# Expert results stored by an indirect store with one index per row, into a table that lies over scratch arrays

## The chip, the cores and the metric

The kernel runs on one core of a Trainium2 chip, in one launch. The metric is the device time of an execution in microseconds (us). The kernel before took 1542.76 us, the median of three runs (1533.67, 1542.76 and 1543.29).

## What is computed

One layer of a hybrid decoder runs over 1024 prompt tokens and 64 sample tokens (8 sequences of 8), 1088 tokens of width 1024 in all. A projection feeds eight RWKV-7 heads (a recurrence per token) and eight heads of dilated windowed attention; an output projection and a residual follow. Then comes the part that the change is about:

- A router picks for each token one of 4 groups of experts and in it 2 of 8 gated-MLP experts, with two weights. The layer adds the two weighted results: `acc + c[:, None] * ((silu(hf @ wg) * (hf @ wu)) @ wd)` for each of the 32 experts, where `c` is zero for tokens that did not choose it. 1088 tokens with 2 choices make 2176 pairs of a token and an expert.
- After that a per-layer embedding is gated and added, and a last RMSNorm gives the output.

## The kernel before, in words

Phases 1 to 3 hold the projection, the recurrence and the attention. Their scratch arrays in device memory are made in `dram` (L79): among them `XV`, `KB`, `BB`, `BV`, `AA` and `GG`, each 4 x 128 x 1088 float32, written slab by slab in phase 1 (L366, L367, L373, L424, L430, L438) and read in the recurrence, the last time at about 711 us. All these transfers are issued by the SP queue.

Phase 4 (`phase4_`, L1356) does the output projection, the norm and the routing. Each expert owns 96 slots (`CAP`). The tokens of an expert get its slots in order of their rank, from slot 0 up; matmuls build `pidx`, a 96 x 32 table that holds for each slot and expert the token's number minus 2048, and 0 where the slot has no token. Line L1563 adds 2048 and makes the integer table `idx`: a slot without a token then holds 2048, which is over the last row of `HN` (the normed tokens, 1088 rows of 1024). `cnt` (L1566) counts the tokens of each expert. `overflow` (L1729) reads the counts and branches: only if an expert has more than 96 tokens does the block behind it run.

Phase 5 runs the 32 experts. Its parts are made in `moe_fns` (L1604):

- `gather(e)` (L1609) issues an indirect load on the POOL queue: 96 rows of `HN` by column `e` of `idx` into a tile of 96 partitions, row by partition. It has a bounds check; a row whose index is out of range is not loaded.
- `xt` transposes the gathered rows and splits them into a high and a low part; `gu` does the gate and up matmuls, `act` the activation, `ht` transposes its result, `down(e, j)` does the down matmul for one half of the columns.
- `out(e, j)` (L1657) copies half a result from PSUM to the tile `y` on ACT. After the second half, L1663 issues on the POOL queue a plain store of all 96 rows to rows 96e to 96e+95 of `YE`, a table of 3072 rows of 1024 float32 (L1239). `y` has three buffers.

The weights of an expert (`load_w`, `load_d`: gate and up in four transfers of 512 KB, down in one of 1024 KB) are issued on the SP queue some three experts ahead, into buffers that come free when ACT and DVE have split the weights of an earlier expert. The order of phase 5 is written out by hand in `phase5` (L1680): between `ordered = True` and `ordered = False` each engine and each queue keeps the order of the program. In the turn of expert e the POOL queue gets the store of expert e - 2 (`out(e - 2, 1)`, L1693) and then the gather of expert e + 3 (L1695), and nothing else. In the other phases a planner orders the instructions by priority and by a model of their times. Waits are made from what an instruction reads and writes: of a transfer, the part of a table that its access pattern names.

Phase 6 (`phase6`, L1797) loads for each tile of tokens the residual and, with two indirect loads by `slot` from `YE` (L1810), the two results of each token; it adds them by weight (L1819), and does the gated embedding and the last norm. The matmuls of the embedding (`embed`, L1568) run beside the first of these loads. `slot` names only rows of slots that were given to a token.

## Time and profile before

| | |
|---|---|
| median of three runs | 1542.76 us (1533.67 to 1543.29) |
| the profiled execution's own time | 1534.7 us |
| its span, first to last instruction | 1533.0 us |
| PE busy in the span | 1373.5 us, 90% |
| DVE, ACT, POOL busy | 957.5, 749.3, 375.6 us |
| mean granted TensorE clock | 0.951 |
| bytes read from and written to device memory | 276.00 MB, 104.05 MB |

The profile is one execution as the hardware profiler saw it. Busy times are sums over an engine's instructions. Windows are in us from the start of the span. The 32 stores of L1663 lie between 1078.8 and 1378.4 us.

### The profile page before, as it was taken

To read this page: it belongs to the slowest core of one execution; us is meant where nothing else is said; L and a number is where in the kernel's file an instruction comes from. 1 tells how busy PE (TensorE), PEld (TensorE's weight loads), DVE (VectorE), ACT (ScalarE), POOL (GpSimd) and SP (SyncE) were. 2 spreads that over 40 slices of the span, in tenths; PEclk is the share of its full clock that TensorE was granted. 3 is DMA by queue.
4 is the path that set the end of the run, shared out by engine and by line. 5 is a ranking of instruction groups with operands and counts; after the bars stand their busy time and mean duration, and the time that the engine had idled before them with its cause. 6 is when DMAs were issued, how large, how long until landed. Compare 5 with 4: busy or idle time off the path is not lost. (4 is left out here: it accounts for less than half of the span.)

```text
span 1533.0 us, 24768 instructions
## 1 busy us (share of the span) xinstructions
PE 1373.5 (90%) x9127; PEld 1129.0 (74%) x9128; DVE 957.5 (62%) x2146; ACT 749.3 (49%) x1368; POOL 375.6 (25%) x391
## 2 busy tenths in 40 slices
PE   4899999989789889995799889996999999988996
PEld 4888999989767767775576667884676666656884
DVE  7523664272148675834557554656898899886664
ACT  5544453321244444533355563333887888783322
POOL 8104453000121222343223331111111112102221
PEclk9999999999888989797999999997999999999998
DMA  6145566999578465339888755555999999997551
GB/s 212 42 159 170 170 194 196 318 313 311 160 190 221 132 183 162 115 88 158 137 185 248 260 167 177 198 200 197 382 391 384 388 388 390 372 367 241 188 171 69
DMA packets 254271, 344.63 MB, mean 225 GB/s; under 512 B 103918, under 2 KB 183088, under 8 KB 253617
## 3 DMA queue, kind: packets, MB, share of 16 engines
q1 hardware_dynamic: 209536, 286.37, 57.0%
q0 software_dynamic: 43296, 52.02, 12.2%
q10 hardware_dynamic: 1312, 4.59, 0.8%
q8 instruction: 74, 1.21, 0.3%
q14 instruction: 53, 0.43, 0.1%
HBM read 276.00 MB, written 104.05 MB: 248 GB/s over the span
## 5 line engine op out<-in xcount | busy, mean ns | idle before, releaser
L270 PE MATMUL pj<-hT_hi,wh 128*128 128x384 f32 (+1 forms) x600 | 199.2, 334 | 4.7 <-DVE lora L278 2.7
L270 PE MATMUL pj<-hT_hi,wl 128*128 128x384 f32 (+1 forms) x600 | 199.0, 332 | 0.0
L270 PE MATMUL pj<-hT_lo,wh 128*128 128x384 f32 (+1 forms) x600 | 198.4, 331 | 0.0
L270 PEld LDWEIGHTS pj<-hT_hi,wh 128*128 128x128 f32 x600 | 113.8, 190 | 6.6 <-DVE lora L278 3.0
L270 PEld LDWEIGHTS pj<-hT_hi,wl 128*128 128x128 f32 x600 | 114.0, 190 | 2.4 <-issue 2.2
L270 PEld LDWEIGHTS pj<-hT_lo,wh 128*128 128x128 f32 x600 | 114.2, 190 | 0.6 <-issue 0.2
L690 DVE TENSOR_TENSOR ftmp<-At,X 128x60 f32<-128x60 f32 (+24 forms) x248 | 57.2, 243 | 54.7 <-DMA At<-ABd 18.2
L1611 POOL DMA_INDIRECT x<-HN,idx x32 | 38.3, 1198 | 204.8 <-PE p4t L1624 195.5
L55 DVE TENSOR_TENSOR dl<-draw,dh 128x1024 fp32r<-128x1024 f32 x66 | 80.0, 1216 | 3.6 <-ACT dh L54 3.6
L1095 PE MATMUL pS<-k,q 128*128 128x512 f32 (+2 forms) x192 | 53.7, 393 | 21.7 <-DMA q<-QP 21.1
L54 ACT ACTIVATE dh<-draw 128x1024 fp32r<-128x1024 f32 x66 | 69.0, 1050 | 8.0 <-DMA draw<-in_w_down_dram 8.0
L55 DVE TENSOR_TENSOR wl<-w,wh 128x1024 fp32r<-128x1024 f32 x25 | 35.2, 1408 | 45.0 <-ACT wh L54 44.2
L692 DVE TENSOR_TENSOR X<-X,ftmp 128x60 f32<-128x60 f32 (+24 forms) x248 | 60.4, 256 | 4.2
L779 POOL TENSOR_TENSOR s<-S,pc 128x512 f32<-128x512 f32 x16 | 16.9, 1055 | 180.5 <-DVE S L798 74.3
L1098 DVE CUSTOM_DVE_ANT_0 s<-pS,bias 128x512 f32<-128x512 f32 (+2 forms) x96 | 50.2, 554 | 11.6 <-PE pS L1095 7.9
L1122 ACT ACTIVATE pt<-pxt 128x512 f32<-128x512 f32 (+3 forms) x64 | 32.4, 514 | 50.7 <-PE pxt L1118 50.5
L1118 PE MATMUL pxt<-ident,s 128*128 128x128 f32 x288 | 48.2, 291 | 9.4 <-DVE pt L1120 5.9
L1107 ACT ACTIVATE s<-s,nm 128x128 f32<-128x128 f32 (+7 forms) x64 | 49.2, 770 | 13.3 <-DVE nm L1103 6.8
L1095 PEld LDWEIGHTS pS<-k,q 128*128 128x128 f32 x192 | 32.4, 204 | 30.7 <-issue 22.7
L1348 PE MATMUL p4y<-dh,hh 128*96 128x512 f32 x128 | 54.0, 422 | 0.7 <-ACT hh L54 0.7
L1348 PE MATMUL p4y<-dh,hl 128*96 128x512 f32 x128 | 50.5, 395 | 0.0
L1348 PE MATMUL p4y<-dl,hh 128*96 128x512 f32 x128 | 50.3, 393 | 0.0
(682 smaller groups left out, 3836.0 us busy)
## 6 DMA issues: line engine op xcount, KB each, us to landing
wraw<-in_w_gate_dram SPq DMA_DIRECT2D x64, 512.0 KB
wraw<-in_w_up_dram SPq DMA_DIRECT2D x64, 512.0 KB
draw<-in_w_down_dram SPq DMA_DIRECT2D x32, 1024.0 KB
out_dram<-in_cache_k_win_dram SPq DMA_DIRECT2D x16, 1016.0 KB
out_dram<-in_cache_v_win_dram SPq DMA_DIRECT2D x16, 1016.0 KB
w<-in_w_in_dram SPq DMA_DIRECT2D x25, 512.0 KB
kc<-in_cache_k_win_dram SPq DMA_DIRECT2D x48, 256.0 KB
vc<-in_cache_v_win_dram SPq DMA_DIRECT2D x48, 256.0 KB
```

Of the source, the lines that this page charges most:

```text
L54: self.hi = self.o(e.activation(hi, src, AF.Copy) if e is nc.scalar else e.tensor_copy(hi, src))
L55: return self.o((lo_eng or nc.vector).tensor_tensor(lo, src, hi.bitcast(F32), op=ALU.subtract))
L270: nc.tensor.matmul(p[:, :nn], a[:, k, :], b[:, k, n0:n0 + nn], start=(m == 0), stop=(m == 23))
L690: nc.vector.tensor_tensor(o, At[:, t, t + 1:32][:, :, None].to_broadcast([128, m, c]), X[:, t, None, 0:c].to_broadcast([128, m, c]), op=AL ...
L692: nc.vector.tensor_tensor(X[:, t + 1:32, 0:c], X[:, t + 1:32, 0:c], o, op=ALU.add)
L1095: nc.tensor.matmul(ps[:, :n], q[:, a, i * 128:(i + 1) * 128], k[:, c0:c0 + n], start=(a == 0), stop=(a == 1))
L1098: nc.vector.tensor_tensor_reduce(s[:, c0:c0 + n], ps[:, :n], bias[:, bo:bo + n], 1.0, -3e38, ALU.add, ALU.max, m)
L1107: ex = nc.scalar.activation(s[:, :nb * 128], s[:, :nb * 128], AF.Exp, bias=nm, accum_out=den)
L1118: nc.tensor.transpose(px[:, b, :], s[:, (b0 + b) * 128:(b0 + b + 1) * 128], self.ident)
L1122: nc.scalar.activation(pt[:, b0:b0 + m, :], px[:, :m, :], AF.Copy)
L1348: self.o(self.nc.tensor.matmul(p, a[x][:, k, :], w, start=(k == 0 and q == 0), stop=(k == kn - 1 and q == 2)))
L1611: d = nc.gpsimd.indirect_dma_start(out=X[e][:n], out_offset=None, in_=self.HN, in_offset=bass.IndirectOffsetOnAxis(ap=self.idx[:, e:e + 1] ...
```

## The change

Three things are done.

1. `YE` is no table of its own any more. The six scratch arrays of the recurrence become slabs of one array `R6` of 6 x 4 x 128 x 1088 float32 (3342336 numbers), and `YE` is a view of its first 3072 x 1024 numbers, which covers the first five slabs and part of the sixth.
2. The constants get a column with the partition's number. After `idx`, two small DVE operations on 96 x 32 build `row`: the slot's row in `YE` (partition + 96 e), plus 3072 where `pidx` is not negative, which is where the slot has no token.
3. The store of L1663 becomes an indirect store on the same queue, with the rows of `y` as source, column `e` of `row` as the index and a bounds check at 3071: a row with an index of 3072 or more is not stored. Its destination, as the instruction names it, is the whole of `YE`.

```diff
-        self.XV = t("XV", [4, 128, T])
+        self.R6 = t("R6", [6, 4, 128, T])
+        self.XV = self.R6[0]
...
-        self.KB = t("KB", [4, 128, T])
-        self.BB = t("BB", [4, 128, T])
+        self.KB = self.R6[1]
+        self.BB = self.R6[2]
...
-        self.BV = t("BV", [4, 128, T])
-        self.AA = t("AA", [4, 128, T])
-        self.GG = t("GG", [4, 128, T])
+        self.BV = self.R6[3]
+        self.AA = self.R6[4]
+        self.GG = self.R6[5]
...
+    row[:, 149] = j
...
-        self.YE = d.tile([NE * CAP, D], F32, name="YE")
+        self.YE = self.R6.rearrange("s p q t -> (s p q t)")[0:NE * CAP * D].rearrange("(r c) -> r c", c=D)
...
+        self.row = c4.tile([CAP, NE], I32, name="row")
...
-        irk, tid = rc[:, 172:172 + CAP], rc[:, 268:277]
+        irk, tid, row = rc[:, 172:172 + CAP], rc[:, 268:277], rc[:, 277:278]
...
         nc.vector.tensor_scalar(self.idx, pidx[:CAP, 0:NE], float(FREE), None, op0=ALU.add)
+        free = p4.tile([CAP, NE], F32, name="free")
+        nc.vector.tensor_scalar(free, pidx[:CAP, 0:NE], 0.0, float(NE * CAP), op0=ALU.is_ge, op1=ALU.mult)
+        nc.vector.scalar_tensor_tensor(self.row, free, row[:CAP], ist[:CAP], op0=ALU.add, op1=ALU.add)
...
-                self.o(nc.gpsimd.dma_start(self.YE[e * n:e * n + n, :], y[:n]))
+                self.o(nc.gpsimd.indirect_dma_start(out=self.YE, out_offset=bass.IndirectOffsetOnAxis(ap=self.row[:, e:e + 1], axis=0),
+                                                    in_=y[:n], in_offset=None, bounds_check=NE * CAP - 1, oob_is_err=False))
```

## Rows read from the trace of the kernel before

**Rows 1.** The page: the span in 40 slices (PE busy, DMA busy and GB/s).

```profile
PE   4899999989789889995799889996999999988996
...
DMA  6145566999578465339888755555999999997551
GB/s 212 42 159 170 170 194 196 318 313 311 160 190 221 132 183 162 115 88 158 137 185 248 260 167 177 198 200 197 382 391 384 388 388 390 372 367 241 188 171 69
```

**Rows 2.** Busy times by stretch; the columns are given in the first line, the last three being the granted TensorE clock, the busy share of the DMA engines and GB/s.

```profile
core 0: us, PE busy (x) PEld busy (x) DVE busy (x) ACT busy (x) POOL busy (x), PEclk, DMA share, GB/s
...
1097.00:1106.20 9.20, 9.20 (x48) 6.54 (x47) 8.99 (x12) 8.28 (x13) 1.57 (x3) 1.00 1.02 385
1078.77:1333.73 254.96, 241.61 (x1197) 169.10 (x1196) 231.11 (x285) 213.46 (x312) 46.76 (x52) 1.00 1.02 386
1380.00:1460.00 80.00, 76.46 (x349) 61.44 (x350) 52.46 (x64) 28.63 (x51) 24.78 (x23) 0.97 0.66 217
```

**Rows 3.** The chain of work that ended last, in order of time (start us, us, what), in the middle and at the end of phase 5.

```profile
1097.49 2.76 PE p4g L1348 x12
...
1106.64 2.77 PE p4g L1348 x12
...
1248.62 15.35 DMA wraw<-in_w_up_dram
...
1302.69 14.96 DMA wraw<-in_w_up_dram
...
1378.38 3.49 DMA YE<-y
1381.93 0.52 issue
1382.50 0.16 issue
1382.66 2.70 POOL y L1810
1385.36 0.30 issue
1385.66 4.44 DMA y<-YE,slot
```

**Rows 4.** The waits of the SP queue from 1078 to 1385 us: in total, how often, the longest.

```profile
SPq L1305 <- DVE hl L55: 70.8, 27, 3.8
SPq L1305 <- DMA draw<-in_w_down_dram: 59.9, 21, 3.8
```

**Rows 5.** DMA traffic from 1078 to 1332 us by queue: packets, MB, share of the time of 16 engines (q0 is POOL's queue, q1 SP's), and two of the issues with KB each and the median us from issue to landing.

```profile
q1 hardware_dynamic: 21658, 80.29, 82.1%
q0 software_dynamic: 5824, 17.59, 19.4%
...
YE<-y POOLq DMA_DIRECT2D x26, 384.0 KB, 7.3
x<-HN,idx POOLq DMA_INDIRECT x26, 7.7
```

**Rows 6.** POOL's queue in order of time (start us, us, what): the gather and the store of one turn, the gather of the next turn, and the last two stores.

```profile
1096.38 0.97 POOL L1611 DMA_INDIRECT x<-HN,idx  x1 [7.21 <-PE p4t L1624]
1098.42 0.55 POOL L1663 DMA_DIRECT2D YE<-y  x1 [1.06 <-ACT y L1661]
1105.53 0.97 POOL L1611 DMA_INDIRECT x<-HN,idx  x1 [6.56 <-PE p4t L1624]
...
1371.52 0.51 POOL L1663 DMA_DIRECT2D YE<-y  x1 [7.98 <-ACT hh L54]
1378.38 0.51 POOL L1663 DMA_DIRECT2D YE<-y  x1 [6.35 <-ACT y L1661]
```

**Rows 7.** DMA traffic in two short stretches, after the gather issued at 1096.38 and before any packet of the store issued at 1098.42: from 1100.2 to 1100.3, then from 1100.2 to 1100.72 us.

```profile
DMA packets 23, 0.03 MB, mean 287 GB/s; under 512 B 16, under 2 KB 16, under 8 KB 23
...
q0 software_dynamic: 14, 0.00, 7.9%
...
q0 software_dynamic: 43, 0.06, 31.7%
```

**Rows 8.** GB/s in 40 slices of 0.5 us each, from 1290 to 1310 us.

```profile
GB/s 418 418 418 410 451 385 426 418 369 426 344 352 361 303 401 320 385 475 410 402 410 410 459 418 385 377 410 377 344 320 320 320 246 270 352 401 426 426 426 401
```

**Rows 9.** All gathers of L1611, then all stores of L1663: duration of an issue in ns (least, median, most), and us from the issue to the landing.

```profile
L1611 POOL DMA_INDIRECT x<-HN,idx x32: 956/975/2007, 1052.4 to 1331.7; - x32
...
DMA to landing us min/median/max: 4.5/7.7/9.6
...
L1663 POOL DMA_DIRECT2D YE<-y x32: 505/548/559, 1078.8 to 1378.4; - x32
...
DMA to landing us min/median/max: 3.5/7.2/8.8
```

**Rows 10.** DVE in order of time at the end of phase 4: the line that makes `idx`, and the last one before the branch; and the first gather on POOL.

```profile
1051.97 0.17 DVE L1563 TENSOR_SCALAR idx<-p4g 96x32 int32<-96x32 f32 x1
...
1052.22 0.13 DVE L1741 CAST ci<-mx 1x1 int32<-1x1 f32 x1
...
1052.44 1.06 POOL L1611 DMA_INDIRECT x<-HN,idx  x1 [7.02 <-DVE ci L1741]
```

**Rows 11.** The SP queue in phases 1 to 2 (four writes to four parts of one scratch table, then the next load), and the stores of `X` with their median us to landing.

```profile
276.65 3.76 SPq L627 DMA_DIRECT2D ABd<-LAB  x4
280.51 0.65 SPq L600 DMA_DIRECT2D bb<-BB  x1
...
X<-x POOLq DMA_DIRECT2D x7, 512.0 KB, 2.9
```

## The prediction, made before the changed kernel was run

> **What bounds the kernel now.** I read the page's slices first: PE is busy almost throughout, but from slice 29 on (1073 to 1380 us) the DMA engines are full as well, at 367 to 391 GB/s [rows 1]. That is phase 5, the stage of the change. The table by stretch then says how close the two limits lie. Where the weights were there in time, one turn of an expert is 9.15 us, from 1097.49 to 1106.64, and PE is busy in all of it [rows 2, 3]. From the first store at 1078.77 to the one at 1333.73 there are 26 turns in 254.96 us, 9.81 each, with PE busy 241.61 us, 9.29 a turn, and a DMA share of 1.02 [rows 2]. So over this stretch transfers, not PE, set the pace; the chain of waits names whom it waits for, the weight loads, with single pieces of 15 us [rows 3]. The SP queue's own waits add how they are held back: for buffers that DVE frees, but 59.9 us in 21 waits for the landing of an earlier load [rows 4]. A load has landed when the slowest of its engines has finished.
>
> **What the change removes.** First the size. From 1078 to 1332 us POOL's queue moved 17.59 MB [rows 5]. 26 stores of 96 rows of 4096 B are 10.22 MB; the other 7.37 MB are 26 gathers, 69.2 rows each. An indirect transfer thus leaves out empty slots already, and 26.8 of the 96 rows of a store hold no token. The change takes away 26 x 26.8 x 4096 B = 2.85 MB of 98 MB in this stretch. At 386 GB/s [rows 2] that is 7.4 us, if every engine gets an equal part of it.
>
> I do not think it does. The engines are 16, the rows 96: six rows each if they are dealt out in blocks. The gather shows the blocks. It was issued at 1096.38; in 0.1 us from 1100.2 its queue shows 14 packets and 0.00 MB, that is 14 empty ones, and 43 packets by 1100.72 with only 0.06 MB, some 15 full rows [rows 7]. Fourteen is twice six skipped rows and a completion. If the skipped rows were spread evenly, each engine would begin with its four full rows. Slots fill from 0 up, so the empty rows are the last 27: four engines get nothing, a fifth about half, and eleven their full six rows. Over a turn, a full engine carries 3.146 MB of weights / 16 = 48 packets of 4 KB, 6 rows of the gather and 6 of the store, 60; the four others 54. After the change these four carry 48 and the full ones still 60. The rates agree that the light ones already run dry: while the queues hold work the slices swing between 418 to 475 GB/s and dips to 246 to 320 [rows 8], and the lowest is 59% of 418. Work is taken from engines that have nothing to do. I therefore cost the relief at 0 to 7.4 us and take 1 us, nearest to nothing, for a little less crowding on the way to memory; the 2% to 3% of bytes saved would buy no more where the slow engines' lists are as long as before.
>
> The Trainium skill, page "DMA: Bandwidth & Descriptors", section "Issuing engines are not separate DMA queues", says that transfers of all queues run on the same 16 engines and interleave. Taken alone it would turn every byte saved into time, and the sum would be 6.4 us lower; the dips in the slices show that one total for the 16 engines isn't the limit here.
>
> **What it adds, step by step.**
> - The issue on POOL. An indirect load takes 0.97 us against 0.55 for the plain store, at most 2.01 [rows 9]. No indirect store is in the trace; the gather is the nearest row. 0.4 us more per turn (up to 1.5) lie in POOL's pauses: it waits 6.6 to 7.2 us before each gather and 1.06 before each store [rows 6], and is busy 46.76 of 254.96 us [rows 2]. Cost 0; if that cover went, 26 x 0.4 = 10 us.
> - The wait for the store before. Each plain store names its own rows. Now each names the whole table, so each must wait until the one before has landed, and behind it on POOL stands the gather of expert e + 3. A plain store lands 7.2 us after its issue, 8.8 at most; a gather 7.7, 9.6 at most [rows 9]. Turns are 9.15 to 9.81 us [rows 2, 3]. So the wait is over before the result is ready in nearly every turn; a rare 0.5 us is covered by the three buffers of `y`. At the last pair the distance is only 6.86 us [rows 6], and there the wait may show: 0 to 0.8 us, I take 0.3. The first store also waits for the last readers of the scratch, over since 711 us: nothing.
> - The last store. It is on the chain: 3.49 us from issue to landing, then the first loads of phase 6 [rows 3]. As an indirect one it issues 0.4 us longer and lands like the fastest gather, 4.5 us [rows 9], against 3.49: 1.0 us together, with -0.3 (fewer rows) to 2.5 (the slowest issue, 1.5 more) as bounds. Behind it stand the loads by `slot`, DVE's additions (which block the copies of the embedding) and PE, which is busy 76.46 of 80 us there [rows 2], so not all of the delay reaches the end. I take 0.7.
> - Two DVE operations of the size of `idx`, 0.17 us each [rows 10], 0.2 to 0.4 us in all. They stand ahead of the branch, behind which the first gather waits [rows 10]. Weight loads behind the branch bound the next stage, so it counts: 0.3.
> - The common array. The writes and reads of the six arrays in phases 1 to 2 name disjoint slabs and keep their waits: 0. The row for it is that four writes to parts of one table go out in 3.76 us, 0.9 apart [rows 11], less than the 2.9 us that a store needs to land on an idle queue [rows 11]. If the cover of disjoint slabs were gone, 24 writes at 2.9 us would be 70 us on SP.
> - The planner may order phases 4 and 6 a little differently around the new instructions; no row prices that, and I allow 4 us either way.
>
> Sum: -1.0 + 0.3 + 0.7 + 0.3 = +0.3 us on the profiled 1534.7, so 1535.0. The profiled run lies 8.1 us under the median of 1542.76, and the three runs themselves spread over 9.6, so the change is smaller than what one kernel does by itself. Against the median the forecast is **1543 us**.
>
> **The rivals.**
> A. *The bytes count.* The rows of an indirect store could be dealt to the engines otherwise than those of the gather, or crowding at memory rather than single engines be the limit. For it: the full DMA share and the rate that hardly varies over a whole stretch [rows 1, 2]. Against: rows 7 and 8. A turn would shrink from 9.81 to 9.52 us, still above PE's 9.15, so all of 7.4 us would come back: 1543 - 6.4 = about 1537. Chance 0.17.
> B. *The wait for the store before sets the pace (slower).* If an indirect store lands more than 9.8 us after its issue, store, landing, next store becomes a closed ring on POOL, and the gathers stand in it. Landing at 10.4 us would cost 26 x 0.6 = 16 us, 1559. Against: the gathers, issued on the same queue amid the same loads, land at 7.7 us [rows 5], 2 us short of the point; for it, their worst of 9.6 [rows 9]. The Trainium skill, page "DMA: Bandwidth & Descriptors", section "Two DMAs through the same engine are not ordered", says that only the completion semaphore orders two transfers, the same queue doesn't. By that rule the ring is real and can't be had for free; how long it is no row here shows. Chance 0.06.
> C. *The common array adds waits in phases 1 and 2*, up to 70 us on SP, of which PE-bound phase 1 would hide most: about 1560. Against it rows 11. Chance 0.02.
> D. *Empty rows are stored after all*, because the bounds check is not met: 12.6 MB as before, only the additions remain, 1544. The gathers' 69 rows speak against it. Chance 0.02.
>
> The forecast itself, within about 5 us of no change, gets 0.73.
>
> **How the numbers follow.** The range takes the forecast, whichever level of the runs shown comes out, rival A and the planner's 4 us: from 1533.67 less about 4 to 1543.29 and the upper bounds of the additions (2.5 + 0.8 + 0.4) and 2 of the planner's: 1530 to 1549. B and C lie outside. One per cent, 15 us, is about what a measurement of this kernel tells from no change. Faster by more needs twice rival A: 0.04, mostly for runs on different levels. Slower by more is B, C and a bad order: 0.08. Within: 0.88.
>
> **What would show it.** Right: in the stretch of phase 5, POOL's queue moves about 14.7 MB instead of 17.59, the turns stay at 9.7 to 9.8 us, the stores' issues grow to about 1 us and nobody waits for a store's landing but phase 6; the dips in the slices grow deeper. Rival A: turns of 9.5 us and a last store some 7 us sooner against the first. Rival B: POOL's waits before stores name the landing of `YE`, and turns grow with it. The forecast is wrong if a load of weights lands sooner with the light engines relieved, or if the ring closes.

## The result, and the profile after

The changed kernel took 1555.28 us, the median of seven runs (1547.86 to 1557.04), and the kernel before 1536.31 beside it (1531.06 to 1543.29). The ratio is 1.0110 with a 95% interval of 1.0080 to 1.0139: **slower, by about 17 us**, outside the range of the prediction. The profiled execution has a span of 1554.1 us against 1533.0.

The page of the changed kernel, the lines that answer to [rows 1]:

```profile
PE   4999999999788888968699889987999999888996
DMA  6145558897776555474978656648999999977541
GB/s 209 55 157 176 182 156 257 290 337 251 214 201 171 154 156 151 116 122 98 171 216 239 229 154 208 224 157 280 366 352 361 370 367 358 348 263 257 191 145 68
```

The DMA engines are as full as before in phase 5 (slices 29 to 35), but they move 348 to 370 GB/s where they moved 372 to 391. Up to phase 5 nothing was lost: the first store starts at 1079.44 us, before at 1078.77. From the last store (1400.75, before 1378.38) to the end it is 153.4 us against 154.6. **All of the loss lies between the first and the last store.** The traffic of that stretch, 1079 to 1345 us, against [rows 5]:

```profile
q1 hardware_dynamic: 22029, 81.67, 83.9%
q0 software_dynamic: 5600, 14.07, 16.0%
...
R<-y,row POOLq DMA_INDIRECT x25
```

The empty rows are indeed skipped: POOL's queue moves 14.07 MB instead of 17.59. How the turns of the experts went is seen in the busy times by stretch (columns as in [rows 2]). The first line reaches from the first store to the copy of expert 26's result, the others are single turns, from one end of ACT's copy of a result to the next, and the sum is that of the 22 turns from expert 4 to expert 26:

```profile
1079.44:1345.00 265.56, 248.64 (x1197) 172.76 (x1196) 231.26 (x285) 213.96 (x313) 66.20 (x51) 0.97 1.00 361
...
1124.93:1134.08 9.15, 9.15 (x47) 6.41 (x46) 8.78 (x12) 8.34 (x13) 1.98 (x2) 1.00 1.03 361
1134.08:1145.89 11.81, 9.12 (x45) 6.10 (x43) 8.43 (x12) 8.11 (x14) 3.50 (x2) 1.00 1.01 354
1145.89:1157.26 11.37, 11.36 (x49) 7.97 (x50) 9.59 (x12) 8.22 (x13) 1.46 (x2) 0.85 0.98 349
...
1319.39:1333.63 14.24, 9.74 (x46) 6.36 (x46) 8.79 (x12) 8.11 (x13) 3.75 (x3) 1.00 0.95 328
1333.63:1344.99 11.36, 11.35 (x49) 7.91 (x50) 9.58 (x12) 8.21 (x13) 1.45 (x2) 0.85 1.00 362
sum 229.21, PE 212.29 PEld 146.87 DVE 196.40 ACT 181.34 POOL 58.93; mean PE 9.65 PEld 6.68 DVE 8.93 ACT 8.24 POOL 2.68
```

The same stretches of the kernel before:

```profile
1153.07:1164.88 11.81, 9.29 (x46) 6.24 (x44) 8.60 (x12) 8.11 (x14) 1.94 (x2) 1.00 1.02 379
1164.88:1174.75 9.87, 9.39 (x46) 6.50 (x46) 8.84 (x12) 8.11 (x13) 1.93 (x2) 1.00 1.02 386
...
sum 217.02, PE 204.78 PEld 143.09 DVE 196.07 ACT 180.68 POOL 39.63; mean PE 9.31 PEld 6.50 DVE 8.91 ACT 8.21 POOL 1.80
```

Both kernels begin phase 5 with weights in hand and run 9.15 us a turn; then the weights are late and turns become uneven. Over the 22 turns the changed kernel is 12.2 us slower, and these have two parts. PE stands idle 229.21 - 212.29 = 16.9 us instead of 12.2, that is 4.7. And PE is busy 7.5 us longer with the same matmuls. In four turns its granted clock is 0.85 of full speed on the mean, a part of the turn at the lower of the two levels (1.2 instead of 2.4 GHz): such a turn takes 11.4 us instead of 9.15 with PE busy nearly throughout, 8.9 us for the four. Each follows directly on a turn in which PE stood idle, for 1.8 to 4.5 us. So these four stalls were paid twice, once as a wait and once as a slower clock. The clocks of all runs say the same: 0.9424 of full speed on the mean over the seven runs after, 0.9452 to 0.9471 over five groups of 17 to 35 runs of the kernel before.

The other 9 us lie behind expert 26. POOL's queue there (as in [rows 6]):

```profile
1343.24 0.96 POOL L1619 DMA_INDIRECT x<-HN,idx  x1 [12.36 <-PE p4t L1632]
1344.51 1.74 POOL L1671 DMA_INDIRECT R<-y,row  x1 [0.30 <-issue]
...
1386.19 1.83 POOL L1671 DMA_INDIRECT R<-y,row  x1 [6.79 <-ACT dh L54]
1393.02 4.09 POOL L1671 DMA_INDIRECT R<-y,row  x1 [4.99 <-ACT whh L54]
1400.75 0.91 POOL L1671 DMA_INDIRECT R<-y,row  x1 [3.64 <-ACT ple L1609]
```

Here the text ahead of the prediction has to be corrected. It says that POOL's queue gets the store of expert e - 2 and then the gather of expert e + 3. In the trace of before the gather is issued first, 2.04 us ahead of the store [rows 6]: the hand-written order did not hold between these two, the planner chose. In the changed kernel, where each store waits for the one before, the planner put a second gather ahead of a store at two places; from the fourth store on, stores run one turn behind their results, from the sixth on two, and eight are left behind the last gather instead of six. They go out one landing apart, and the last starts 6.4 us after its rows are ready at 1394.3. The stores themselves, against [rows 9]:

```profile
L1671 POOL DMA_INDIRECT R<-y,row x32: 911/1581/4087, 1079.4 to 1400.7; - x32
...
DMA to landing us min/median/max: 6.6/6.8/7.1
```

An issue takes 1.58 us in the median, not 0.97. Of the landings this trace has only two. In `own_all_gfirst` and `after_gfirst`, two kernels below whose traces have all 32, they take 8.0 and 7.9 us in the median, against 7.2 for the plain store. So five things could have cost the 1.1%: the late stores, the indirect store by itself, the common array, the table's place over the scratch, the skipping.

### The profile page after: what moved, and what is told of

Its sections match the earlier page's. It is cut to its first block, busy times and chain, and to the rows that moved or that the text cites. A ratio compares the mean times of both kernels' runs of the same rounds, so it can differ in the third digit from the quotient of the medians.

```text
span 1554.1 us, 24806 instructions
## 1 busy us (share of the span) xinstructions
PE 1385.1 (89%) x9127; PEld 1135.3 (73%) x9128; DVE 957.2 (62%) x2148; ACT 749.6 (48%) x1368; POOL 400.2 (26%) x391
## 4 chain that ended last, share of the span: by engine, by line
PE 45%; DMA 23%; DVE 15%; issue 8%; ACT 4%; SPq 3%; POOL 2%; POOLq 0%; DVEq 0%; ACTq 0%
PE pj L272 13%; PE p4y L1351 10%; DMA wraw<-in_w_up_dram 4%; DMA wraw<-in_w_gate_dram 3%; DMA q<-QP 3%; PE p4g L1351 2%; PE po L1062 2%; PE pS L1097 2%; PE pxt L1120 2%; DMA At<-ABd 2%; DVE X L694 2%; DMA QP<-qlo 2%; DMA R<-y,row 2%; DVE ftmp L692 1%; DMA AR<-ARd 1%
## 5 line engine op out<-in xcount | busy, mean ns | idle before, releaser
L1619 POOL DMA_INDIRECT x<-HN,idx x32 | 35.3, 1103 | 214.3 <-PE p4t L1632 204.9
L1671 POOL DMA_INDIRECT R<-y,row x32 | 49.4, 1543 | 56.8 <-ACT dh L54 20.9
L781 POOL TENSOR_TENSOR s<-S,pc 128x512 f32<-128x512 f32 x16 | 16.9, 1055 | 179.0 <-DVE S L800 70.1
```

Source lines behind the costliest of these rows:

```text
L1619: d = nc.gpsimd.indirect_dma_start(out=X[e][:n], out_offset=None, in_=self.HN, in_offset=bass.IndirectOffsetOnAxis(ap=self.idx[:, e:e + 1] ...
L1671: self.o(nc.gpsimd.indirect_dma_start(out=self.YE, out_offset=bass.IndirectOffsetOnAxis(ap=self.row[:, e:e + 1], axis=0), in_=y[:n], in_of ...
```

## Experiments

Ratios are to the kernel before on the same chip, with 95% intervals. The names of theories in the expectations: W is the wait with the place in the queue, L the table's place in memory, I the indirect store itself. "22 turns" is the sum over experts 4 to 26 as above: the turns, PE's idle time in them, and the number of turns with a granted clock under 0.97.

```
kernel                  ratio    22 turns   PE idle   low-clock turns
before                  1        217.0      12.2      0
first_plain             1.0010   218.6      12.6      1
chain_plain             0.9981   215.1      9.7       1
before_inorder          1.0045   221.3      14.9      0
own_all_inorder         1.0047   225.1      18.8      0
alias_plain             1.0042   225.3      16.4      3
r6_only                 1.0050   225.7      13.0      5
after_inorder           1.0064   225.6      19.2      0
own_all_rows            1.0083   224.5      13.1      4
own_all_gfirst          1.0100   229.2      19.4      2
all_rows                1.0104   223.4      13.4      3
changed kernel          1.0110   229.2      16.9      4
after_gfirst            1.0116   232.1      22.0      2
plain_gather            1.0030   216.5      11.1      1
plain_gather_own_all    1.0109   229.5      20.5      1
spread_plain            0.9915   208.3      5.3       0
spread_plain_2          0.9932   208.9      5.9       0
spread_after_inorder    0.9990   210.8      5.9       0
spread_after_gfirst     0.9986   211.4      7.2       0
spread_own_all_inorder  1.0016   215.6      10.2      0
```

The turns are those of one profiled execution each; `first_plain` turned out to be a second measurement of the kernel before, and shows how far two executions differ (1.6 us in these turns, 11.6 us in all). The profiled executions of `spread_after_inorder` and `spread_after_gfirst` were 10 and 12 us faster than the medians of these kernels, so their turns do not stand for their ratios.

**Are the late stores the cause, and do the skipped rows pay?** `chain_plain` is the kernel before with each plain store held until the one before has landed, `all_rows` the change without its skipping.

```diff
-                self.o(nc.gpsimd.dma_start(self.YE[e * n:e * n + n, :], y[:n]))
+                d = self.o(nc.gpsimd.dma_start(self.YE[e * n:e * n + n, :], y[:n]))
+                self.hold(d, getattr(self, 'last_store', None))
+                self.last_store = d
```

> The kernel before with one thing added: each plain store waits until the store before it has landed. All 96 rows are stored, the table is its own, no row table. The planner then puts POOL's queue in the same order as in the changed kernel. Theory W expects the loss of the change here, with nothing indirect in it: ratio 1.008 to 1.016, last store minus first store 315 to 325 us, and stores that leave up to 20 us after their rows are ready. Theories L and I expect 1536, ratio 1.000 within 0.004.

Measured 0.9981 (0.9956 to 1.0005). The planner gave it the order of the changed kernel: POOL's queue shows gather and store back to back, with stores two turns late (18.7 us after their rows on the mean from the sixth store to the 26th, worked out from ACT's copies).

```profile
1192.74 0.98 POOL L1611 DMA_INDIRECT x<-HN,idx  x1 [7.94 <-PE p4t L1624]
1193.71 0.57 POOL L1663 DMA_DIRECT2D YE<-y  x1
```

So with plain stores neither the wait nor the late store costs anything. Theory W falls.

```diff
-        nc.vector.tensor_scalar(free, pidx[:CAP, 0:NE], 0.0, float(NE * CAP), op0=ALU.is_ge, op1=ALU.mult)
+        nc.vector.tensor_scalar(free, pidx[:CAP, 0:NE], 0.0, 0.0, op0=ALU.is_ge, op1=ALU.mult)
```

> The change with the rows of empty slots stored too (their index is that of their own slot, so nothing is skipped): the 29% of the bytes come back, all waits stay. Theory W, with the engines that carry the last rows idle anyway, expects the time of the change within 3 us: 1552 to 1558, ratio 1.009 to 1.014 against before. If the bytes counted, it would be some 7 us over the change: 1562, ratio 1.017.

Measured 1.0104 (1.0058 to 1.0151), the changed kernel again: 2.85 MB fewer bytes in phase 5 bought nothing that can be measured. The 7 us that were possible are 0.5%, no more than the width of this interval on either side; two more pairs, in the section on why the prediction was wrong, point the same way.

**The order restored.** `after_inorder` pins the gather of expert e + 3 behind the store of expert e - 2 (gathers and stores alternate, the gather last); `after_gfirst` restores exactly the order of the kernel before, by emitting the gather first and pinning the store behind it and the next gather behind the store.

```diff
-                gather(e + 3)
+                with self.tc.issue_after(self.last_store.ins):
+                    gather(e + 3)
```

and for `after_gfirst`, whose gathers are emitted ahead of `out(e - 2, 1)`, besides that

```diff
-                self.o(nc.gpsimd.indirect_dma_start(out=self.YE, out_offset=bass.IndirectOffsetOnAxis(ap=self.row[:, e:e + 1], axis=0),
+                with self.tc.issue_after(self.last_gather.ins):
+                    self.last_store = self.o(nc.gpsimd.indirect_dma_start(out=self.YE, out_offset=bass.IndirectOffsetOnAxis(ap=self.row[:, e:e + 1], axis=0),
...
```

> The change with one thing added: the gather of expert e+3 is queued behind the store of expert e-2, so gathers and stores alternate in POOL's queue and no store is put behind two gathers. The wait of each store for the landing of the one before stays. If the wait alone costs, the time stays at 1550 to 1557. If the place in the queue is what makes the stores two turns late (theory W, its second half), most of the loss goes: 1536 to 1542, ratio 1.000 to 1.004, last store minus first store 300 to 306 us. Theory I expects no change against the changed kernel.

> The change itself, with the order of gathers and stores of the kernel before restored. If order is all that the change lost beside the common array (0.5%): 1.004 to 1.006. If the indirect store costs by itself as well: 1.007 to 1.011, the order restored gains little.

Measured 1.0064 (1.0040 to 1.0088) and 1.0116 (1.0068 to 1.0164). The first ratio lies between the two that were forecast, the second just above the higher one. With the order of before, stores start 0.4 us after their rows on the mean, 1.4 at most, and the ring at the end is gone, but not a microsecond comes back. So the planner's order was not the cause; only the other order, gather behind store, helps, by some 7 us (the two intervals overlap a little), and it has no turn at a lower clock.

**The indirect store of every row.** `own_all_inorder`, `own_all_rows` and `own_all_gfirst` store every row through an index (the one of `all_rows`) into a table of its own, at its old place: the bytes of before, and the old addresses of `HN` and the table. They differ in the order of gathers and stores: gather behind store, the planner's, that of the kernel before. They are made from the changed kernel, and the edit puts back the table alone: the six scratch arrays are still slabs of the common array. Two expectations below say that the common array is left out; it is not. So the control with plain stores is `r6_only`, further below, which has the common array and the order of before. `before_inorder` has plain stores and the gather behind the store, without the common array.

```diff
-        self.YE = self.R6.rearrange("s p q t -> (s p q t)")[0:NE * CAP * D].rearrange("(r c) -> r c", c=D)
+        self.YE = d.tile([NE * CAP, D], F32, name="YE")
```

> The kernel before with its own table, every row stored, only that the store is indirect and that the gather of the third expert after it is queued behind it. Leaves out of the change: the common array and the skipping of empty rows. Theory I (the indirect store itself costs: 1.5 us of issue instead of 0.55, landing of about 8 us, a ring of landings among the last stores): about +0.2% or more, 1540 to 1546, the last store 5 to 10 us later than 1378.4, mean 4 KB packet of the weight queue back at about 169 ns. Theory L (all that is not queue order is the place of the table): 1.000, the last store within 2 us of 1378.4.

> As the run beside it, but with the order of gathers and stores that the planner chooses: stores two turns late. If queue order costs only together with the slow landing of indirect stores: about 0.45% above its neighbour (7 us), stores 18 to 20 us behind their rows, six to eight stores after the last gather, one landing apart. If queue order costs only in the place of the common array: equal to its neighbour within 0.2%.

> The kernel before, with plain stores and its own table, only that the gather of expert e + 3 is queued behind the store of expert e - 2, as in the two runs with stores in order. It is the control for the order alone. In the runs with indirect stores in order (1.0047 with the own table) the slow stretch of a turn (about 300 GB/s, packets of over 200 ns) goes with the packets of the gather, and there the gather's packets stand alone after the store's; before, store and gather overlap. If that order costs: 1.003 to 1.005, and the indirect store itself is nearly free. If the indirect store costs by itself (issue, descriptors, landing): 0.998 to 1.002 here.

> Indirect stores of every row into the table's own place, with gathers and stores in exactly the order that the kernel before has on POOL's queue (the gather of expert e + 3, then the store of expert e - 2, and so on). Leaves out of the change: the common array and the skipping. If the indirect store is free and the costs so far were order: 0.998 to 1.002. If it costs by itself in this order (issue of 1.5 us, slower weight packets while it is made ready): 1.004 to 1.008, steady turns of 10.2 us and more.

Measured 1.0047 (1.0022 to 1.0072), 1.0083 (1.0052 to 1.0113), 1.0045 (1.0022 to 1.0068) and **1.0100 (1.0069 to 1.0130)**. The last has almost all of the change's loss. But it differs from the kernel before by two things, the indirect store and the common array, and `r6_only`, with the common array and plain stores, has 1.0050 (1.0029 to 1.0071). So about half of the 1.0% comes with the array; the other half, 0.5% or some 8 us, comes with the indirect store. These are the pairs in which both kernels have the common array (with the gather behind the store there is no such control):

```
indirect stores          plain stores           difference
own_all_gfirst  1.0100   r6_only      1.0050    0.50%
own_all_rows    1.0083   r6_only      1.0050    0.33%
changed kernel  1.0110   alias_plain  1.0042    0.68%
all_rows        1.0104   alias_plain  1.0042    0.62%
after_gfirst    1.0116   alias_plain  1.0042    0.74%
```

Each difference is uncertain by some 0.4% or more, and they share two controls; the intervals of a pair fail to touch only for the changed kernel and `alias_plain`. All five lie on the same side: with the array there anyway, the indirect store costs 0.3% to 0.7%, 5 to 11 us. With the gather behind the store, by contrast, the indirect store and the array together add nothing to what that order costs anyway (1.0047 beside 1.0045).

The traces show what happens in a turn: GB/s in 40 slices of half a microsecond, 1190 to 1210 us, and POOL's issues in them, for the kernel before:

```profile
GB/s 410 418 434 393 434 418 418 426 385 410 385 410 361 369 262 328 328 352 426 410 418 451 401 418 426 401 418 369 361 352 385 451 418 402 385 295 352 336 361 418
...
1191.97 0.98 POOL L1611 DMA_INDIRECT x<-HN,idx  x1 [6.56 <-PE p4t L1624]
1194.00 0.55 POOL L1663 DMA_DIRECT2D YE<-y  x1 [1.06 <-ACT y L1661]
1201.36 2.00 POOL L1611 DMA_INDIRECT x<-HN,idx  x1 [6.81 <-PE p4t L1624]
```

and for `own_all_gfirst`:

```profile
GB/s 385 434 369 377 320 279 295 229 270 270 410 418 418 401 434 410 418 426 418 401 426 401 393 401 385 401 295 262 320 295 279 410 426 426 418 410 434 385 418 401
...
1187.59 0.96 POOL L1619 DMA_INDIRECT x<-HN,idx  x1 [6.16 <-PE p4t L1632]
1190.42 1.64 POOL L1672 DMA_INDIRECT YE<-y,row  x1 [1.86 <-ACT y L1669]
1198.20 1.10 POOL L1619 DMA_INDIRECT x<-HN,idx  x1 [6.15 <-PE p4t L1632]
```

Between gathers the engines move 400 to 430 GB/s. Some 4.5 us after the issue of a gather, when its rows are under way, this falls to 230 to 350 for 2.5 to 3 us. The engines are not idle then. In these two stretches of `own_all_gfirst`, one inside the fall and one behind it, their busy share (columns as in [rows 2]) is the same:

```profile
1192.00:1195.00 3.00, 3.00 (x16) 2.11 (x15) 2.27 (x4) 1.78 (x4) 0.06 (x1) 1.00 1.02 277
1195.00:1198.00 3.00, 3.00 (x19) 2.24 (x18) 3.00 (x3) 3.00 (x5) 0.00 (x0) 1.00 1.02 415
```

What changes is the time of a packet: the weight queue's 4 KB packet takes 205 to 236 ns on the mean in the middle of such a fall, in this kernel and in the kernel before, and 160 to 172 away from it. Over 23 turns (the gathers of experts 3 to 25) the means are, worked out from all packets of 4 KB:

```
us after the gather's issue  4.0  4.5  5.0  5.5  6.0  6.5  7.0  7.5
before            GB/s       385  372  311  317  317  338  376  398
r6_only           GB/s       372  332  306  303  314  320  359  394
alias_plain       GB/s       373  338  301  303  304  317  368  399
own_all_gfirst    GB/s       388  343  292  283  288  304  327  377
plain_gather      GB/s       402  291  298  319  317  390  407  423
plain_gather_own  GB/s       346  284  296  285  299  316  388  414
spread_plain      GB/s       417  392  302  293  334  392  409  411
before, packets of POOL's queue       11.2 18.0 16.4 17.4 16.9 17.5 17.7 16.3
r6_only, the same                     11.4 14.9 15.8 16.5 15.9 14.3 18.8 17.1
own_all_gfirst, the same               8.5 14.0 13.9 13.6 12.4  7.3 11.7 13.7
```

In the kernel before the rows of the store, issued 2 us after the gather, run in the same stretch. In `own_all_gfirst` they come later: 6.5 us after the gather's issue POOL's queue has 7.3 packets in half a microsecond instead of 17.5, and the stretch is deeper and longer. Measured against 410 GB/s a turn loses 233 KB there before and 339 KB in `own_all_gfirst`. But the kernels with the common array and plain stores lose 290 KB (`r6_only`) and 288 (`alias_plain`), although their stores' rows run beside the gather's as before. So 57 of the 106 KB come with the array, and 49 with the indirect store: 0.12 us a turn at 410 GB/s, some 4 us over 32 turns, half of that pair's 8. In the 22 turns of the table PE idles 6.4 us more in `own_all_gfirst` than in `r6_only` and is busy some 3 us less, with two turns at a low clock instead of five. The cost does not lie in POOL's time: POOL still waits for ACT's copy before each store. That it lies in the later rows is what the packets suggest, and not shown.

In the planner's order the cost lies elsewhere. The 22 turns of `all_rows` (223.4 us) and `own_all_rows` (224.5) are no longer than with the array and plain stores (225.3 and 225.7); from the end of expert 26's copy to the end of the span they take 209.4 and 214.3 us, where `alias_plain` takes 203.6 and `r6_only` 202.4. The changed kernel has some of both, 229.2 us in the turns and 209.1 behind them. With one profiled execution each these parts are rough. Theory I stands for about half of the loss, its mechanism open.

**Whose is the slow stretch?** In the last pair the gather is a plain load of 96 rows that follow one another (other rows than the tokens', 27 more a turn), in the order of the kernel before. `plain_gather` has plain stores and no common array; `plain_gather_own_all` has indirect stores and, like the other kernels with a table of its own, the common array.

```diff
-            d = nc.gpsimd.indirect_dma_start(out=X[e][:n], out_offset=None, in_=self.HN,
-                                         in_offset=bass.IndirectOffsetOnAxis(ap=self.idx[:, e:e + 1], axis=0),
-                                         bounds_check=T - 1, oob_is_err=False)
+            r0 = e % 11 * n
+            d = nc.gpsimd.dma_start(X[e][:n], self.HN[r0:r0 + n, :])
```

> The kernel before, its order of gathers and stores unchanged, but the gather is a plain load of 96 rows of HN that follow one another: other rows than the tokens', so the experts compute on other data, and 27 more full rows a turn (2.7% more bytes). If the slow stretch belongs to reading scattered rows through an index: it goes, weight packets stay near 160 ns, steady turns fall to 9.3 to 9.6 us in spite of the bytes, 0.988 to 0.994. If it belongs to 96 rows of HN on the same engines, whatever names them: turns of 10.0 us and more, 1.000 to 1.005.

> As its neighbour with the plain load in place of the gather, but the store is indirect, of every row, into the table's own place. If an indirect store costs by what it does to the gather's stretch (its packets come too late to run beside it): within 0.3% of its neighbour. If it costs by its own issue and packets: again 0.7% to 1.0% above its neighbour.

Measured 1.0030 (1.0004 to 1.0057) and 1.0109 (1.0077 to 1.0140). GB/s from 1200 to 1220 us, `plain_gather` with its gather issued at 1203.89:

```profile
GB/s 410 402 434 418 434 410 410 426 401 418 401 426 401 418 442 410 385 303 295 303 320 410 426 418 402 434 410 434 385 410 434 418 426 418 401 319 303 303 328 393
...
1203.89 0.51 POOL L1612 DMA_DIRECT2D x<-HN  x1 [8.84 <-PE p4t L1623]
1205.90 0.51 POOL L1663 DMA_DIRECT2D YE<-y  x1 [1.51 <-ACT y L1660]
```

and `plain_gather_own_all`, where the next store even waits for the landing of the one before:

```profile
GB/s 410 418 434 410 418 393 418 401 418 418 393 279 295 279 295 279 393 410 434 410 418 418 410 426 377 418 418 401 410 426 410 303 279 295 320 295 344 393 418 393
...
1201.15 0.53 POOL L1620 DMA_DIRECT2D x<-HN  x1 [6.16 <-PE p4t L1631]
1203.58 1.62 POOL L1671 DMA_INDIRECT YE<-y,row  x1 [1.90 <-ACT y L1668]
1211.37 0.53 POOL L1620 DMA_DIRECT2D x<-HN  x1 [6.17 <-PE p4t L1631]
1214.03 0.94 POOL L1671 DMA_INDIRECT YE<-y,row  x1 [2.14 <-DMA YE<-y,row]
```

The slow stretch stays without an index: it belongs to reading 96 rows of `HN`, not to reading them indirectly. And the indirect store and the common array together cost 0.8% once more, with a stretch longer by the same 105 KB (223 and 328); this pair cannot tell the two apart. In both pairs there is a gap in the store's rows behind the gather's; a kernel that only delays a plain store by those microseconds was not tried.

**The table's place.** `alias_plain` has the common array and the table over it, with plain stores; `r6_only` the common array, the table behind `HN` as before; `first_plain` declares the table first and changes nothing else.

```diff
+        self.R6 = t("R6", [6, 4, 128, T])
...
-        self.YE = d.tile([NE * CAP, D], F32, name="YE")
+        self.YE = self.R6.rearrange("s p q t -> (s p q t)")[0:NE * CAP * D].rearrange("(r c) -> r c", c=D)
```

> Only the common array: YE lies over the recurrence's scratch as in the change, the stores are the plain ones of before, and there is no row table. Theory W (the wait of each store for the store before, and the place of the stores in POOL's queue) expects no change: 1536 us, ratio 1.000 within 0.004, last store minus first store 299 to 303 us as before. Theory L (the place of the table in memory slows the weight loads, whose packets are longer after the change) expects most of the loss here: 1550 us or more, ratio 1.008 to 1.014. Theory I (the indirect store itself) expects 1536.

> The kernel before with the six scratch arrays as slabs of one array, plain stores, and the table of results on its own behind HN as before. If the common array costs in phases 1 to 3 or by the planner's order: 1.003 to 1.006, first gather later or the end later with turns as before. If the cost of 0.4% seen with the common array and plain stores is that of the table lying over it: 0.998 to 1.002 here.

> The kernel before with plain stores and separate scratch arrays, but the table of results is declared as the first array in device memory, where the changed kernel has it; nothing lies over anything else. If it is the place of the table, whatever lay there before: like the common array with plain stores, 1.003 to 1.006, turns of 10.1 us, mean 4 KB packet of the weight queue about 172 ns. If the place costs nothing: 0.998 to 1.002.

Measured 1.0042 (1.0011 to 1.0073), 1.0050 (1.0029 to 1.0071) and 1.0010 (0.9992 to 1.0028). The first lies between the theories: W and I expected no change, L twice as much or more. Beside the second it shows that to lay the table over the scratch adds nothing; what costs 0.4% to 0.5%, 6 to 8 us, is there with the common array alone. The second has the number that was forecast for a cost of the array, but not the reason: its turns are not those of before. The compiler places arrays by itself and gave the last the addresses of the kernel before. In `r6_only` `HN` and the table keep their addresses too, and every engine and queue has the order of the kernel before; one instruction at 890 us has a wait more. What differs is this:

```profile
1207.15:1216.30 9.15, 9.15 (x48) 6.50 (x47) 8.94 (x12) 8.22 (x12) 1.53 (x2) 1.00 1.03 386
1216.30:1225.44 9.14, 9.06 (x46) 6.24 (x45) 8.55 (x12) 8.34 (x13) 1.54 (x2) 1.00 1.02 382
1225.44:1237.67 12.23, 9.33 (x46) 6.29 (x44) 8.62 (x12) 8.12 (x14) 2.34 (x2) 1.00 1.00 371
1237.67:1249.04 11.37, 11.36 (x49) 7.93 (x50) 9.59 (x12) 8.23 (x14) 1.53 (x2) 0.85 1.00 378
...
sum 225.69, PE 212.64 PEld 148.00 DVE 196.53 ACT 180.94 POOL 38.10; mean PE 9.67 PEld 6.73 DVE 8.93 ACT 8.22 POOL 1.73
```

PE waits no longer than before (13.0 us against 12.2); the stalls come in larger pieces, and after five of them the clock is low for a turn, 11.0 us in all over turns of 9.15. So Theory L falls as worded: `r6_only` moves no address that phase 5 uses and loses as much. Why the stalls fall together there is open. With the array's part known, the sum comes out: 0.4% to 0.5% with the array and 0.3% to 0.7% with the indirect store make the change's 1.1%. But `r6_only` also warns: an edit that leaves phase 5 as it was can cost 0.5% there, so a single difference of that size between two kernels does not show its cause.

The turns of `own_all_inorder` are the opposite: each a little late, none at a low clock.

```profile
1203.18:1213.38 10.20, 9.39 (x46) 6.51 (x46) 8.88 (x13) 8.11 (x12) 2.65 (x2) 1.00 1.03 384
1213.38:1223.48 10.10, 9.40 (x46) 6.51 (x46) 8.84 (x12) 8.11 (x12) 2.62 (x2) 1.00 1.02 375
```

**Dealing the empty rows to all engines.** In the spread kernels rank r gets slot 6 (r mod 16) + r / 16, rounded down, instead of slot r, so that the empty slots lie evenly among the 96 rows.

```diff
-    row[:, 44:140] = np.arange(96)
+    row[:, 44:140] = np.arange(96) % 6 * 16 + np.arange(96) // 6
...
-            nc.vector.scalar_tensor_tensor(self.slot[:, i0:i0 + nb, :].rearrange("p t a -> p a t"), rk, CAP - 1.0, e0,
-                                           op0=ALU.min, op1=ALU.add)
+            nc.vector.tensor_scalar(rm, rk, CAP - 1.0, None, op0=ALU.min)
+            nc.vector.tensor_scalar(q, rm, 0.0625, -0.46875, op0=ALU.mult, op1=ALU.add)
+            nc.vector.tensor_scalar(q, q, 12582912.0, None, op0=ALU.add)
+            nc.vector.tensor_scalar(q, q, -12582912.0, -95.0, op0=ALU.add, op1=ALU.mult)
+            tt(q, q, e0, op=ALU.add)
+            nc.vector.scalar_tensor_tensor(self.slot[:, i0:i0 + nb, :].rearrange("p t a -> p a t"), rm, 6.0, q,
+                                           op0=ALU.mult, op1=ALU.add)
```

> The kernel before with plain stores and its own table, but a token's rank within its expert is turned into a slot so that the empty slots lie evenly among the rows (rank r gets slot 16 times the remainder of r by 6, plus r divided by 6, or its mirror), so that the empties, which the gather already skips, are shared by all 16 DMA engines. If the full engines set a turn (prediction's step: 60 packets a turn on the full ones): 1.7 packets of 60 fewer a turn, 0.28 us by 32 turns, minus 5 to 9 us, 1528 to 1534, ratio 0.994 to 0.997. If bytes alone set it: no change, ratio 0.999 to 1.001.

> The spread kernel with plain stores once more (0.9915 before), beside the other three: 0.989 to 0.994. It is also the version that is to beat both kernels.

> The change with its stores in order and the empty slots spread evenly over the rows, so that gathers and stores both skip rows of every DMA engine alike. If dealing of rows to engines hid the gain of the skipped rows (prediction's step): 3.4 of 60 packets fewer a turn on the full engines, about 0.5 us by 26 to 32 turns, minus 8 to 16 us against the same kernel unspread (1.0064), so 0.996 to 1.001. If the indirect store itself sets the turn: within 0.2% of 1.0064.

> Indirect store of every row into the table's own place, stores in order, with empty slots spread evenly over the rows. Against the same with plain stores (0.9915): if the indirect store costs whatever the dealing of empty rows, by its issue or by its place in the queue, again about 0.5% more, 0.995 to 0.998; if its cost came from the full engines of the gather, equal within 0.2%, 0.990 to 0.993. Against the spread change in order (0.999), which skips the empty rows and has the table over the scratch: equal or lower means that skipping still buys nothing where every engine skips alike.

> The change in the order of the kernel before, with the empty slots spread evenly over the rows, so that gathers and stores skip rows of every DMA engine alike. If the skipped bytes pay once they are dealt evenly and order and indirect store cost nothing: 0.3 to 0.5% under the spread kernel with plain stores beside the common array's 0.5%, so about level with its neighbour, 0.990 to 0.994. If the indirect store eats that: 0.996 to 1.000, 0.5% and more above its neighbour.

`spread_plain`, the kernel before and nothing else changed, gave 0.9915 (0.9882 to 0.9949) and in its second run 0.9932 (0.9901 to 0.9962): 10 to 13 us **faster than the kernel before**, more than was expected, and so faster than both kernels. Its gather, here issued at 1199.77, slows the engines for 1.5 us instead of 2.5 to 3:

```profile
GB/s 369 426 401 410 418 418 442 410 410 418 336 270 279 401 401 418 426 434 418 401 410 451 418 418 401 418 451 410 418 295 320 287 418 410 401 451 393 426 401 410
...
1199.77 1.37 POOL L1617 DMA_INDIRECT x<-HN,idx  x1 [7.25 <-PE p4t L1630]
1209.65 0.97 POOL L1617 DMA_INDIRECT x<-HN,idx  x1 [7.21 <-PE p4t L1630]
```

The other three: the change in order 0.9990 (0.9962 to 1.0018), indirect stores of all rows in order 1.0016 (0.9998 to 1.0035), the change in the order of before 0.9986 (0.9950 to 1.0021). Even where every engine skips alike, the kernels with indirect stores lie 0.5% or more above those with plain stores of all rows; they all have the common array, and two of them the other order, so that this is not the store's alone. Between skipping and not skipping in order the intervals overlap.

## Why the prediction was wrong

**What bounds the kernel** was right: transfers with PE close behind. **What the change removes** was right in size: a relief of 1 us of 7.4, and the runs with and without it are level. Three pairs say so: 1.0110 with skipping and 1.0104 without (the change and `all_rows`), 1.0116 and 1.0100 in the order of before, 1.0064 and 1.0047 in the other order. In the last two the table's place differs too, which costs nothing by `alias_plain` and `r6_only`. Rival A wanted 0.4% to 0.5% less with skipping, and falls. The Trainium skill, page "DMA: Bandwidth & Descriptors", section "Issuing engines are not separate DMA queues", says that the transfers of all queues run on the same 16 engines and interleave; taken alone, it would have given rival A's 7.4 us, and no pair shows them. The reason given, that the last rows fall on few engines, fits the spread kernels, where 10 to 13 us come out and 5 to 9 were expected; the lists of single engines were not looked at, so that it is likely, not shown. Rival D falls as well: 14.07 MB, with 14.7 forecast.

**The steps that failed are two terms put at nothing: "The issue on POOL ... Cost 0" and "The common array ... 0".** The first priced the indirect store as a plain one with a longer issue, found the issue covered, and had no term for its rows in the traffic. POOL's cover was there (66.20 of 265.56 us busy), although the issue was longer than bounded, 1.58 us in the median and 4.09 at most against 0.97 and 2.01. Yet with the common array on both sides kernels with indirect stores take 0.3% to 0.7%, 5 to 11 us, more than those with plain stores. In the order of before their rows reach the engines later, the stretch of a turn in which packets are slow loses 49 KB more, and PE waits 19.4 us instead of 13.0 in the 22 turns (`own_all_gfirst` and `r6_only`); that the one causes the other is argued. In the planner's order, the changed kernel's, a part of it lies behind expert 26, and the cause there stays open.

The second term priced waits on SP in phases 1 and 2, and there nothing was lost, so rival C's place was wrong: the first gather is at 1052.5 us in `r6_only` and at 1052.4 before. But with plain stores the array costs 0.4% to 0.5%, 6 to 8 us, in phase 5, where the prediction did not look for it: five turns at a low clock in `r6_only`, and a slow stretch that loses 57 KB more. Why an array that phase 5 does not touch does this stays open.

[rows 8] showed the dips of 246 to 320 GB/s; they were read as engines with nothing to do. For the second of them the table by stretch says otherwise:

```profile
1304.00:1307.50 3.50, 3.50 (x19) 2.44 (x18) 2.57 (x4) 2.22 (x3) 0.00 (x0) 1.00 0.90 310
1307.50:1310.00 2.50, 2.50 (x16) 1.82 (x15) 1.37 (x3) 2.24 (x3) 0.00 (x0) 1.00 1.02 416
```

The rate is down by a quarter, the busy share by an eighth: some engines do stand idle, and packets are slower, 187 ns instead of 160. The dip comes with the rows of the gather issued at 1300.68, as in the other turns. With that reading the time at which the store's rows come would have been seen as worth a term.

**The second miss is a missing step:** that a stall costs PE its clock. [rows 2] give 1.00 for phase 5 of the kernel before, and nothing in them shows a fall; four turns at 0.85 took 8.9 us over 9.15 each, and PE was busy 7.5 of the 12.2 us longer.

**The wait for the store before** was placed right, at a cost of nothing: `chain_plain`. Rival B forecast 1559 and came near in number only: no ring closed on POOL in phase 5, since gathers waited for PE; it closed among the last stores, 6.1 us at the end that `after_gfirst` removed without a gain. **The order of POOL's queue** was read wrongly from the code, although [rows 6] show the gather first. **The planner** was given 4 us for phases 4 and 6, not for phase 5, where it moved stores by two turns; that cost nothing. **The last store**, +0.7: not told apart.

## What to carry to other kernels

Bytes taken from a full DMA phase need not come back as time: leaving out the last rows of each store bought nothing here, dealing the gather's empty rows evenly bought 10 to 13 us. A transfer through an index is not a plain one with a longer issue; ask when its packets come and what ran beside them. Give each part of a change a kernel of its own, and take the control from the same base: the kernels for the indirect store kept the common array, and beside the kernel before they make the store look twice as dear. Where PE is within a few per cent of the transfers, look at the granted clock turn by turn: here large stalls often cost a slower turn as well, small even ones did not.

## What the runs showed of the hardware

While 96 rows of `HN` are read, plain or through an index, the 16 engines together fall from 410 to some 280 to 320 GB/s with their busy share near 1; while a plain store's rows run alone they do not: in `before_inorder`, with the store's rows alone, from 4.0 to 6.0 us after its issue, the rate is 407 to 418. Whether that is the table's place, that all its rows were written shortly before, or the tile that is written was not tried. Two programs with the same order and the same addresses in phase 5 (`r6_only` and the kernel before) differ by 0.5%; in the profile the difference is turns at a low clock, and the mean granted clock of the runs is 0.9449 and 0.9470. And PE's clock did not fall after every stall: in the kernel before it stood idle for 2.52 us in the turn from 1153.07 and went on at 1.00. What decides that the runs don't show.
